# Eight of the feed-forward's column pairs by seven products instead of five, with the hidden pairs' low halves made by accumulating transfers

## The chip, the cores and the metric

The kernel runs on one core of a Trainium2 chip. The metric is device time in microseconds (us) of one execution; lower is better. The engines are named as in the profile: PE (TensorE, with PEld for its weight loads), DVE (VectorE), ACT (ScalarE), POOL (GpSimd) and SP (SyncE, which here only issues transfers).

## The reference, cut to what matters

One transformer-like layer on 512 tokens of 1024 features, in float32. Attention comes first; its code is the same in both kernels. The change lies in the convolutional gated feed-forward at the end:

```python
def conv_glu(x, w_up, conv_w, conv_b, w_down):      # x: (1, 512, 1024), w_up: (1024, 5632)
    hid = x @ w_up
    hid = lax.conv_general_dilated(hid, conv_w[:, None, :], ..., padding=((CONV_WIDTH - 1, 0),),
                                   feature_group_count=2 * D_FF) + conv_b
    gate, up = hid[..., :D_FF], hid[..., D_FF:]      # D_FF = 2816 columns each
    return (jax.nn.silu(gate) * up) @ w_down         # w_down: (2816, 1024)
```

## The kernel before

**Precision.** Every float32 operand is kept as two parts, `hi` (rounded to the matmul's format, cast by ACT) and `lo` (the rest, a subtraction on DVE). One product is three matmuls: hi by hi, hi by lo, lo by hi.

**Up-projection.** The 2816 gate columns and the 2816 up columns are cut into 22 column pairs of 128 + 128 (`up0` to `up21`). For each, SP loads 1 MB of weights into one of two slots (`raw`), ACT and DVE split them into `whi` and `wlo` (two buffers each), and PE multiplies them by the normalized tokens (`hth`, `htl`). While PE is at column pair j, the splits of j+1 are made and the load of j+3 is issued as soon as its slot is free (`run_chunk`, `split_gen`). An ordinary pair (`up_body`) is 48 matmuls of 512 columns (two outputs, eight slices of the features, three matmuls each). Five of the 22 pairs, those in `SEVEN`, are multiplied as 2x2 blocks by seven products instead of eight (`up_seven`): 84 matmuls of 256 columns. For this, four sums of the weight blocks are formed on DVE (`block_sums`, in `sx`) and split as well (`wxh`, `wxl`), and four sums of the token blocks are formed once and split (`token_sums`: the tiles `xT` and `ts`). The convolution, the gate and their product (`conv`, `gate`, `up_fin`) run on ACT and DVE while PE is at the next pair; the result of column pair j is one quarter of the tile `ub`.

**Hidden pairs.** Two column pairs make one hidden pair i (`pair_sums`). Its results are summed into blocks for a seven-product scheme of the down-projection, and split into `ax` (hi and lo, 1 MB) and `ay` (hi and lo, 768 KB): four sums on DVE, four casts on ACT, four subtractions on DVE. POOL then writes `ay` of the hidden pairs 0 to 6 out to DRAM (`ayd`) and reads them back after column pair 18 and in the down-projection (`fetch`).

**Down-projection.** `dn0_i` (24 matmuls with `ax` of hidden pair i) for all eleven hidden pairs, then `dn1_i` (18 matmuls with `ay`). 

**What sets the order.** The tile scheduler places the instructions of each engine in one fixed order; at run time an engine takes them in that order and waits on semaphores for the others. A transfer is queued by the engine that issues it, behind the waits in front of it there.

Of the kernel before, what the change touches and what calls it, by code (L numbers as in the profile page):

```python
# [8 lines left out]
F32 = mybir.dt.float32  # L9
# [53 lines left out]
SEVEN = (5, 8, 11, 14, 17)  # L63
# [3 lines left out]
def block_kernel(ctx: ExitStack, tc: tile.TileContext, x, xt, params, g2, rbx, wts, wd0, wd1, out):  # L67
# [45 lines left out]
    def load(i, parts=1):  # L113
# [6 lines left out]
        if i >= FIRST_DN:  # L120
            n = i - FIRST_DN
            if n < NP:
                SP.dma_start(raw, wd0[n])
            else:
                late["load"] = (SP.dma_start(raw[:, 0:1024], wd1[n - NP]),)
            yield
            return

        cuts = [0, *parts, 8] if isinstance(parts, tuple) else [8 * j // parts for j in range(parts + 1)]
        for a, b in zip(cuts, cuts[1:]):  # L130
            sl = slice(256 * a, 256 * b)
            SP.dma_start(raw[:, sl], wts[i, :, sl])
            yield
# [39 lines left out]
    def block_sums(i):  # L173

        b = raws[i].rearrange("p (b c) -> p b c", c=512)
        sx = late["pool"].tile([P, 1536], F32, tag="sx", name=f"sx_{order[i]}")
        late["sx"] = sx
        s1, s2, s4 = (sx[:, 512 * j:512 * (j + 1)] for j in range(3))
        V.tensor_tensor(s1, b[:, 1], b[:, 3], op=ALU.add)
        yield  # L180
        V.tensor_tensor(s2, s1, b[:, 0], op=ALU.subtract)
        yield
        V.tensor_tensor(s4, b[:, 2], s2, op=ALU.subtract)
# [4 lines left out]
    def split_seven(i, raw, hi, lo):  # L188

        key = order[i]  # L190
# [3 lines left out]
        sx = late["sx"]  # L194
        for j, (h, l, src) in enumerate(((hi[:, 0:1024], lo[:, 0:1024], raw[:, 0:1024]),
                                         (wh[:, 0:1024], wl[:, 0:1024], sx[:, 0:1024]),
                                         (hi[:, 1024:2048], lo[:, 1024:2048], raw[:, 1024:2048]),
                                         (wh[:, 1024:1536], wl[:, 1024:1536], sx[:, 1024:1536]))):
            A.copy(h, src)
            V.tensor_tensor(l, src, h.bitcast(F32), op=ALU.subtract)  # L200
            if j < 3:
                yield
# [39 lines left out]
    def run_chunk(key, body, pieces=4):  # L242

        sp = split_gen(pos[key] + 1, pieces)
        for _ in body(*splits.pop(key)):
            next(sp, None)
            yield
# [17 lines left out]
    ayd = dram.tile([7, P, 1536], F32, tag="ayd", name="ayd")  # L265

# [354 lines left out]

    def soft_b(h, t, ps):
# [247 lines left out]
    def pair_sums(i):  # L870
# [5 lines left out]
        if i < 8:  # L876
            ax = fp.tile([P, 2048], F32R, tag="ax", name=f"ax{i}", bufs=8)
            ay = fp.tile([P, 1536], F32R, tag="ay", name=f"ay{i}")
        elif i == 8:

            ax = fp.tile([P, 2048], F32R, tag="ts", name=f"ax{i}", bufs=4)
            ay = fp.tile([P, 1600], F32R, tag="wxh", name=f"ay{i}")[:, 0:1536]
            keep[0] = fp.tile([P, S], F32, tag="hg", name="t2_0")
# [367 lines left out]
```

## Time and profile before

| | |
|---|---|
| runs of the kernel | 725.96, 726.20, 726.39 us; median 726.2 us |
| the profiled execution | 726.66 us, of which the span from the first to the last instruction is 724.9 us |
| busy in the span | PE 718.6, PEld 627.5, DVE 565.4, ACT 401.5, POOL 53.6 us |
| granted PE clock | 1.00 of full speed |
| transfers | 100.91 MB, 139 GB/s over the span |

A busy time counts overlapping instructions once. PE's matmuls overlap each other, so their pace is read from the distance of their starts, not from the duration of one; the same holds, to a lesser degree, for DVE and ACT. In a row of the timeline stand the start, the duration, the engine, the line of the code, the operation with output and inputs, and how many instructions were merged. In a row of the stages stand the stage, its length, and for each engine the busy time and the number of instructions, then the granted clock, the transfer engines' share and GB/s.

### The profile page before, as it was taken

To read this page: it belongs to the slowest core of one execution; us is meant where nothing else is said; L and a number is where in the kernel's file an instruction comes from. 1 tells how busy PE (TensorE), PEld (TensorE's weight loads), DVE (VectorE), ACT (ScalarE), POOL (GpSimd) and SP (SyncE) were. 2 spreads that over 40 slices of the span, in tenths; PEclk is the share of its full clock that TensorE was granted. 3 is DMA by queue.
4 is the path that set the end of the run, shared out by engine and by line. 5 is a ranking of instruction groups with operands and counts; after the bars stand their busy time and mean duration, and the time that the engine had idled before them with its cause. 6 is when DMAs were issued, how large, how long until landed. Compare 5 with 4: busy or idle time off the path is not lost.

```text
span 724.9 us, 10589 instructions
## 1 busy us (share of the span) xinstructions
PE 718.6 (99%) x4019; PEld 627.5 (87%) x4019; DVE 565.4 (78%) x1030; ACT 401.5 (55%) x727; POOL 53.6 (7%) x95
## 2 busy tenths in 40 slices
PE   8999999999999999999999999999999999999997
PEld 8999998888988888888889889889898988888886
DVE  6678867775988888566275799998979985997686
ACT  6675656657767676442254556655545653543541
POOL 2701200000101011000012000000000100000000
PEclk9999999999999999999999999999999999999999
DMA  8632232211313111314536613544335553564563
GB/s 308 250 131 78 83 117 74 74 59 58 118 63 113 59 59 59 136 68 144 195 149 239 203 62 156 186 135 160 118 145 186 181 184 117 173 243 174 177 222 116
DMA packets 24786, 100.91 MB, mean 139 GB/s; under 512 B 2592, under 2 KB 7328, under 8 KB 17184
## 3 DMA queue, kind: packets, MB, share of 16 engines
q1 hardware_dynamic: 21792, 87.00, 33.8%
q0 software_dynamic: 2656, 13.11, 5.0%
q8 instruction: 31, 0.51, 0.3%
q14 instruction: 19, 0.16, 0.1%
q10 hardware_dynamic: 288, 0.14, 0.1%
HBM read 88.44 MB, written 11.80 MB: 138 GB/s over the span
## 4 chain that ended last, share of the span: by engine, by line
PE 98%; DMA 1%; SPq 0%; DVE 0%; ACT 0%; DVEq 0%; issue 0%
PE P L1087 14%; PE p L998 7%; PE pg L254 4%; PE pg L253 4%; PE pg L255 4%; PE pu L254 4%; PE pu L255 4%; PE pu L253 4%; PE qkB L255 2%; PE gB L255 2%; PE qkB L253 2%; PE gA L253 2%; PE gA L254 2%; PE gB L253 2%; PE gA L255 2%; PE qkB L254 2%
## 5 line engine op out<-in xcount | busy, mean ns | idle before, releaser
L253 PE MATMUL pg<-hth,whi_up 128*128 128x512 f32 (+1 forms) x152 | 55.7, 367 | 0.0
L255 PE MATMUL pg<-hth,wlo_up 128*128 128x512 f32 (+1 forms) x152 | 55.7, 366 | 0.0
L254 PE MATMUL pg<-htl,whi_up 128*128 128x512 f32 (+1 forms) x152 | 55.7, 366 | 0.0
L254 PE MATMUL pu<-htl,whi_up 128*128 128x512 f32 (+1 forms) x152 | 55.6, 366 | 0.0
L253 PE MATMUL pu<-hth,whi_up 128*128 128x512 f32 (+1 forms) x152 | 55.6, 366 | 0.0
L255 PE MATMUL pu<-hth,wlo_up 128*128 128x512 f32 (+1 forms) x152 | 55.6, 365 | 0.0
L1087 PE MATMUL P<-whi_dn,ax 128*128 128x512 f32 x176 | 54.4, 389 | 0.0
L149 ACT CAST whi_dn<-raw_dn 128x1024 fp32r<-128x1024 f32 x33 | 34.3, 1051 | 25.5 <-PE P L1087 15.2
L145 DVE TENSOR_TENSOR wlo_dn<-raw_dn,whi_dn 128x1024 fp32r<-128x1024 f32 x33 | 40.0, 1224 | 9.2 <-ACT whi_dn L149 9.1
L228 DVE TENSOR_TENSOR wlo_up<-raw_up,whi_up 128x1024 fp32r<-128x1024 f32 (+1 forms) x40 | 41.2, 1062 | 7.0 <-ACT whi_up L226 7.0
L226 ACT CAST whi_up<-raw_up 128x1024 fp32r<-128x1024 f32 (+1 forms) x40 | 34.5, 917 | 14.7 <-PE pu L254 7.9
L1087 PE MATMUL P<-whi_dn,ay 128*128 128x512 f32 x132 | 40.8, 389 | 0.0
L1087 PEld LDWEIGHTS P<-whi_dn,ax 128*128 128x128 f32 x176 | 33.0, 188 | 6.8
L1087 PE MATMUL P<-wlo_dn,ax 128*128 128x512 f32 x88 | 34.2, 389 | 0.0
L254 PEld LDWEIGHTS pu<-htl,whi_up 128*128 128x128 f32 x152 | 28.6, 188 | 4.7
L253 PEld LDWEIGHTS pu<-hth,whi_up 128*128 128x128 f32 x152 | 28.5, 188 | 4.7
L255 PEld LDWEIGHTS pg<-hth,wlo_up 128*128 128x128 f32 x152 | 28.6, 188 | 4.7
L255 PEld LDWEIGHTS pu<-hth,wlo_up 128*128 128x128 f32 x152 | 28.5, 188 | 4.6
L253 PEld LDWEIGHTS pg<-hth,whi_up 128*128 128x128 f32 x152 | 28.6, 188 | 4.6
L254 PEld LDWEIGHTS pg<-htl,whi_up 128*128 128x128 f32 x152 | 28.6, 188 | 4.5
L633 DVE TENSOR_TENSOR_SCAN aB<-aB,reset 128x127 f32<-128x127 f32 (+3 forms) x32 | 26.0, 817 | 6.7 <-ACT aB L628 6.7
L1087 PEld LDWEIGHTS P<-whi_dn,ay 128*128 128x128 f32 x132 | 24.8, 188 | 5.1
(303 smaller groups left out, 2240.3 us busy)
## 6 DMA issues: line engine op xcount, KB each, us to landing
raw_up<-in_wts SPq DMA_DIRECT2D x22, 1024.0 KB, 4.8
raw_dn<-in_wd SPq DMA_DIRECT2D x11, 1024.0 KB, 4.8
raw_dn<-in_wd SPq DMA_DIRECT2D x11, 512.0 KB, 3.4
ayd<-ay POOLq DMA_DIRECT2D x7, 768.0 KB, 5.2
ay<-ayd POOLq DMA_DIRECT2D x7, 768.0 KB, 6.5
raw_gA<-in_wts SPq DMA_DIRECT2D x4, 1024.0 KB, 4.7
raw_qkB<-in_wts SPq DMA_DIRECT2D x4, 1024.0 KB, 4.8
raw_gB<-in_wts SPq DMA_DIRECT2D x4, 1024.0 KB, 4.7
```

The lines of the kernel that those rows point to most:

```text
L145: chain("halves", V.tensor_tensor(o, x, y, op=op))
L149: chain("casts", A.copy(hi[:, sl], src))
L226: A.copy(hi[:, sl], raw[:, sl])
L228: E.tensor_tensor(lo[:, sl], raw[:, sl], hi[:, sl].bitcast(F32), op=ALU.subtract)
L253: PE.matmul(ps, sh, mh, start=first, stop=False)
L254: PE.matmul(ps, sh, ml, start=False, stop=False)
L255: PE.matmul(ps, sl, mh, start=False, stop=last)
L633: V.tensor_tensor_scan(ar, ar, reset[:, S - n:S - 1][:, ::-1], 1.0, op0=ALU.mult, op1=ALU.max)
L998: PE.matmul(ps, st, mv[:, k, :], start=first and k == 0 and n == 0, stop=last and k == 3 and n == 2, skip_group_check=True)
L1087: chain("products", PE.matmul(dst, st, mv, start=first and n == 0, stop=last and n == 2, skip_group_check=True))
```

## The change

Five things are changed together:

1. `SEVEN` is (6, 8, 10, 12, 14, 16, 18, 20) instead of (5, 8, 11, 14, 17): eight pairs, every second one from the seventh pair on. The splits of the token sums move from column pairs 2 and 3 to 3 and 4.
2. The sums of the weight blocks: only the first (`s1`) has a tile of its own; the other two are formed in place in `raw`, between the splits, so `raw` is read until the last of them.
3. For the hidden pairs 0 to 8 the low half is no longer a subtraction on DVE: ACT writes minus the rounded source into it, and POOL issues a transfer that adds the source onto it (`accum_op=ALU.add`): four such transfers for each hidden pair.
4. The steps of a hidden pair are taken one at a time (`late["todo"]`) along with the next column pair's products. `ay` has two buffers; it is written out by SP instead of POOL, ordered behind one more load of weights. `ax` of hidden pair 0 is written out too (`axd`), its buffer goes to hidden pair 8, and it is read back into another after column pair 20.
5. The reads of `ay` are spread over the down-projection: one after each of `dn0_0`, 2, 3, 5, 6, 8 and `dn1_0`, each waiting for the last load of weights to have landed.

```diff
-SEVEN = (5, 8, 11, 14, 17)
+SEVEN = (6, 8, 10, 12, 14, 16, 18, 20)
...
     def split_seven(i, raw, hi, lo):
...
-        for j, (h, l, src) in enumerate(((hi[:, 0:1024], lo[:, 0:1024], raw[:, 0:1024]),
-                                         (wh[:, 0:1024], wl[:, 0:1024], sx[:, 0:1024]),
-                                         (hi[:, 1024:2048], lo[:, 1024:2048], raw[:, 1024:2048]),
-                                         (wh[:, 1024:1536], wl[:, 1024:1536], sx[:, 1024:1536]))):
+        def part(h, l, c0, src):
+            sl = slice(c0, c0 + src.shape[-1])
+            A.copy(h[:, sl], src)
+            V.tensor_tensor(l[:, sl], src, h[:, sl].bitcast(F32), op=ALU.subtract)
+        part(hi, lo, 0, raw[:, 0:1024])
+        V.tensor_tensor(b[:, 0], s1, b[:, 0], op=ALU.subtract)
+        yield
+        part(wh, wl, 0, s1)
+        part(wh, wl, 512, b[:, 0])
+        yield
+        part(hi, lo, 1024, raw[:, 1024:2048])
+        V.tensor_tensor(b[:, 2], b[:, 2], b[:, 0], op=ALU.subtract)
+        yield
+        part(wh, wl, 1024, b[:, 2])
...
+    def after(ins, others):
+        for o in others:
+            tc.add_manual_dep(ins.ins, o.ins.name, mybir.DependencyInfo(
+                mybir.DependencyClass.Sync, mybir.DependencyReason.DATA), reason="paced")
+        return ins
...
                 A.copy(a[:, sl], src)
-                ins.append(V.tensor_tensor(a[:, n + o:n + sl.stop], src, a[:, sl].bitcast(F32), op=ALU.subtract))
+                if i < 9:
+                    A.activation(lo, src, AF.Copy, scale=-1.0)
+                    G.dma_start(lo, src, accum_op=ALU.add)
+                else:
+                    ins.append(V.tensor_tensor(lo, src, a[:, sl].bitcast(F32), op=ALU.subtract))
...
         if j % 2 == 1 and j // 2 < 9:
-            for step in pair_sums(j // 2):
-                step()
-            if j // 2 < 7:
-                G.dma_start(ayd[j // 2], pairs[j // 2][1].bitcast(F32))
+            i = j // 2
+            late["todo"] += [*pair_sums(i), *[lambda: None] * (6 if i else 0)]
+            if 0 < i < 8:
+                late["todo"].append(lambda: behind(SP.dma_start(ayd[i - 1], pairs[i - 1][1].bitcast(F32)), late["ld"]))
+            if i == 6:
+                late["todo"].append(lambda: behind(SP.dma_start(axd, pairs[0][0].bitcast(F32)), late["ld"]))
...
-            if j in (2, 3):
+            if j in (3, 4):
                 next(late["ts"])
...
-        if j == 18:
-            for i in range(5):
-                fetch(i)
+        if j == SEVEN[-1]:
+            keep[0] = fp.tile([P, S], F32, tag="hg", name="t2_0")
+            ax0 = fp.tile([P, 2048], F32R, tag="ts", name="ax0_", bufs=4)
+            G.dma_start(ax0, axd)
+            pairs[0] = (ax0, None)
...
+            n = ({0: 0, 2: 1, 3: 5, 5: 6, 6: 2, 8: 3}, {0: 4})[s].get(i)
+            if n is not None:
+                fetch(n)
```

How this moves the instructions is shown at three places. The line numbers of the changed kernel differ. In a name the digits next to the letters are the column pair or the hidden pair, those after the last underscore the buffer's.

DVE, at the end of a hidden pair, before (hidden pair 2, while PE is in column pair 7; `st` holds the sums, `L909` are the low halves):

```order
L898 TENSOR_TENSOR st2_4812<-ub_4184 128x256
L909 TENSOR_TENSOR ay2_4811<-ub_4184,ay2_4811 128x256
L899 TENSOR_TENSOR ub_4184<-ub_4184 128x256
L900 TENSOR_TENSOR st2_4812<-st2_4812,ub_4184 128x256
L853 SCALAR_TENSOR_TENSOR cg6_4860<-pg6_4826,par_88,cg6_4860 128x511
L909 TENSOR_TENSOR ax2_4810<-st2_4812,ax2_4810 128x256
L901 TENSOR_TENSOR st2_4812<-ub_4184,st2_4812 128x256
L909 TENSOR_TENSOR ax2_4810<-ub_4184,ax2_4810 128x768
L854 SCALAR_TENSOR_TENSOR cg6_4860<-pg6_4826,par_88,cg6_4860 128x510
L909 TENSOR_TENSOR ay2_4811<-st2_4812,ay2_4811 128x512
```

Sums and low halves alternate here. DVE, the same step now (hidden pair 3, while PE is in column pair 8, which is multiplied by seven products and gives `p6_8`, `p5_8`, `p7_8`):

```order
L1028 TENSOR_TENSOR hu8_4994<-p6_8_4991,hg8_4993 128x256
L939 TENSOR_TENSOR ub_4185<-cg7_4946,ub_4185 128x512
L903 TENSOR_TENSOR st3_5030<-ub_4185 128x256
L1034 TENSOR_TENSOR hg8_4993<-p5_8_4989,hu8_4994 128x256
L904 TENSOR_TENSOR ub_4185<-ub_4185 128x256
L905 TENSOR_TENSOR st3_5030<-st3_5030,ub_4185 128x256
L192 TENSOR_TENSOR wxl_up10_5143<-s1_up10_5049,wxh_up10_5142 128x512
L1038 TENSOR_TENSOR hu8_4994<-p7_8_4990,hu8_4994 128x256
L906 TENSOR_TENSOR st3_5030<-ub_4185,st3_5030 128x256
L1039 TENSOR_TENSOR hu8_4994<-hu8_4994,pc8_4992 128x256
```

The four subtractions into `ax` and `ay` are gone from DVE; the sums now stand between the additions that finish column pair 8.

ACT, at the same steps, before:

```order
L851 ACTIVATE ub_4184<-pu6_4827,par_88 128x512
L867 ACTIVATE cg5_4787<-cg5_4787 128x512
L908 CAST ay2_4811<-ub_4184 128x256
L851 ACTIVATE cg6_4860<-pg6_4826,par_88 128x512
L908 CAST ax2_4810<-st2_4812 128x256
L908 CAST ax2_4810<-ub_4184 128x768
L908 CAST ay2_4811<-st2_4812 128x512
L226 CAST whi_up9_5007<-raw_up9_4858 128x1024 x2
```

The four casts (`L908`) stand ahead of the casts of the next weights. ACT, now (`L914` is the cast to the high half, `L917` the negated write to the low half):

```order
L1031 COPY hg8_4993<-p1_8_4988 128x256
L191 CAST wxh_up10_5142<-s1_up10_5049 128x512
L914 CAST ay3_4987<-ub_4185 128x256
L917 ACTIVATE ay3_4987<-ub_4185 128x256
L914 CAST ax3_4986<-st3_5030 128x256
L917 ACTIVATE ax3_4986<-st3_5030 128x256
L861 ACTIVATE cg8_5103<-hg8_4993,par_88 128x512
L914 CAST ax3_4986<-ub_4185 128x768
L917 ACTIVATE ax3_4986<-ub_4185 128x768
L191 CAST whi_up10_5140<-raw_up10_4980 128x1024 x2
L914 CAST ay3_4987<-st3_5030 128x512
L917 ACTIVATE ay3_4987<-st3_5030 128x512
```

Each cast of a hidden pair has a second pass behind it, and the casts of column pair 10's weights (`whi_up10`) stand behind six of the eight.

SP, the loads of column pairs 8 to 14, before:

```order
L132 DMA raw_up8_4732<-in_wts 128x2048
L132 DMA raw_up9_4858<-in_wts 128x2048
L132 DMA raw_up10_4965<-in_wts 128x2048
L132 DMA raw_up11_5026<-in_wts 128x2048
L132 DMA raw_up12_5136<-in_wts 128x2048
L132 DMA raw_up13_5259<-in_wts 128x2048
L132 DMA raw_up14_5304<-in_wts 128x2048
```

Here SP issues nothing but loads. SP, the same loads now (`ayd` is the copy of `ay` in DRAM):

```order
L129 DMA raw_up8_4763<-in_wts 128x2048
L129 DMA raw_up9_4810<-in_wts 128x2048
L945 DMA ayd_108<-ay0_4439 128x1536
L129 DMA raw_up10_4980<-in_wts 128x2048
L945 DMA ayd_108<-ay1_4595 128x1536
L129 DMA raw_up11_5028<-in_wts 128x2048
L129 DMA raw_up12_5197<-in_wts 128x2048
L945 DMA ayd_108<-ay2_4770 128x1536
L129 DMA raw_up13_5250<-in_wts 128x2048
L945 DMA ayd_108<-ay3_4987 128x1536
L129 DMA raw_up14_5415<-in_wts 128x2048
```

The writes of `ay` stand between the loads, each behind the load that was issued last.

More of the change, by code (lines that the diff above doesn't have):

```diff
@@ L121, in load @@
             n = i - FIRST_DN
[L122 to L125, printed above, removed]
+            late["ld"] = (SP.dma_start(raw, wd0[n]) if n < NP else SP.dma_start(raw[:, 0:1024], wd1[n - NP]),)
             yield
@@ L175, in block_sums @@
         b = raws[i].rearrange("p (b c) -> p b c", c=512)
-        sx = late["pool"].tile([P, 1536], F32, tag="sx", name=f"sx_{order[i]}")
-        late["sx"] = sx
-        s1, s2, s4 = (sx[:, 512 * j:512 * (j + 1)] for j in range(3))
+        s1 = late["s1"] = late["pool"].tile([P, S], F32, tag="s1", name=f"s1_{order[i]}")
         V.tensor_tensor(s1, b[:, 1], b[:, 3], op=ALU.add)
[L180 to L183, printed above, removed]
         yield
@@ L1054, in block_kernel @@
             pass
-        if j == 18:
-            for i in range(5):
-                fetch(i)
+        if j == NF - 1:
+            for step in late["todo"]:
+                step()
+            late["todo"] = []
+        if j == SEVEN[-1]:
[3 more added lines that the diff above has]
+            pairs[0] = (ax0, None)
     BLK = {1: 0, 2: 1, 5: 2, 7: 3, 3: 0, 4: 1, 6: 2}
@@ L1179, in steps1 @@
         for t in range(NT):
-            behind(SP.dma_start(tmp["x"][t // 2][:, t % 2, :], x2d[t]), late["load"])
+            behind(SP.dma_start(tmp["x"][t // 2][:, t % 2, :], x2d[t]), late["ld"])
             if t in (1, 2):
```

45 lines of the change are left out of this document (21 added, 24 removed).

## The prediction, as it was put on record before the changed kernel was run

> **What bounds the kernel now.** I read the page first, then the chain of waits, then PE's starts in the feed-forward, then the busy times by stage, and last the starts on DVE and ACT, which tell what an instruction costs its engine.
>
> ```profile
> PE 718.6 (99%) x4019; PEld 627.5 (87%) x4019; DVE 565.4 (78%) x1030; ACT 401.5 (55%) x727; POOL 53.6 (7%) x95
> PE 98%; DMA 1%; SPq 0%; DVE 0%; ACT 0%; DVEq 0%; issue 0%
> ```
>
> PE is busy in 99% of the span and is 98% of the chain that ended last. Time goes only where PE's own work shrinks, and comes only where PE starts to wait. In the chain by time, a column pair with seven products is one piece:
>
> ```profile
> 435.60 9.89 PE p L998 x84
> 467.28 9.89 PE p L998 x84
> 498.96 9.89 PE p L998 x84
> 615.78 104.94 PE P L1087 x462
> ```
>
> It takes 9.89 us for 84 matmuls, 0.1177 each, three times alike. An ordinary pair follows from two starts, of column pairs 2 and 4:
>
> ```profile
> 402.77 0.40 PE L253 MATMUL pg<-hth,whi_up 128*128 128x512 f32 x1
> 424.56 0.39 PE L253 MATMUL pg<-hth,whi_up 128*128 128x512 f32 x1
> ```
>
> Two pairs take 21.79 us, one takes 10.895 (48 matmuls of 0.227). The chain's period agrees: 467.28 - 435.60 = 31.68 = 9.89 + 21.79, so PE waits nowhere between. By stage (one period, then its parts):
>
> ```profile
> 498.80:530.50 31.70, 31.70 (x182) 27.94 (x181) 28.65 (x45) 18.61 (x30) 1.07 (x2) 1.00 0.35 125
> 435.40:445.30 9.90, 9.90 (x85) 9.86 (x84) 9.90 (x16) 7.00 (x13) 0.54 (x1) 1.00 0.66 260
> 445.30:467.10 21.80, 21.80 (x98) 18.06 (x97) 21.80 (x37) 13.03 (x18) 0.53 (x1) 1.00 0.39 141
> ```
>
> The columns are PE, PEld, DVE, ACT, POOL. DVE is the next engine: full in the two stages around the first seven-product pair, 90% in a later period. The clock is 1.00.
>
> **The change part by part.** *Three more pairs by seven products* remove 3 x (10.895 - 9.89) = 3.02 us from PE. Where the pairs stand changes nothing in that. The Trainium skill, "TensorE: Matmul & The Clock Gate", section "Back-to-back issue gap", gives N/2.4 + 2.5 ns for a matmul of N columns in a stream; by it a pair would shrink from 48 x 215.8 to 84 x 109.2 ns, by 1.19 us, and the three by 3.56. The trace has 227 and 117.7 in their place, and the measured rows decide here.
>
> *DVE and ACT.* Costs are distances of starts in back-to-back rows:
>
> ```profile
> 445.46 0.43 DVE L899 TENSOR_TENSOR ub<-ub 128x256 f32<-128x256 f32 x1
> 445.79 0.43 DVE L900 TENSOR_TENSOR st<-st,ub 128x256 f32<-128x256 f32 x1
> 449.59 1.23 DVE L228 TENSOR_TENSOR wlo_up<-raw_up,whi_up 128x1024 fp32r<-128x1024 f32 x1
> 450.72 0.70 DVE L181 TENSOR_TENSOR sx_up<-sx_up,raw_up 128x512 f32<-128x512 f32 x1
> 451.33 0.70 DVE L185 TENSOR_TENSOR raw_up<-raw_up 128x512 f32<-128x512 f32 x1
> 457.00 0.76 DVE L853 SCALAR_TENSOR_TENSOR cg<-hg,par,cg 128x511 f32<-128x511 f32 x1
> 457.66 0.70 DVE L200 TENSOR_TENSOR wxl_up<-sx_up,wxh_up 128x512 fp32r<-128x512 f32 x1
> 460.72 1.24 DVE L200 TENSOR_TENSOR wlo_up<-raw_up,whi_up 128x1024 fp32r<-128x1024 f32 x1
> ```
>
> So 256 columns cost DVE 0.33, 512 cost 0.60, 1024 cost 1.13, and a convolution step 0.66. From column pair 6 on the pattern is one seven-product and one ordinary pair, 9.89 + 10.895 = 20.79 us of PE. In it DVE has, for the seven-product pair, four block sums (2.40), low halves of 2 x 1.13 + 3 x 0.60 (4.06), five small additions (1.65), four convolution steps (2.64) and one product (0.60): 11.35. The ordinary pair has 2.26 + 2.64 + 0.60 = 5.50, the hidden pair's four sums 1.32. Together 18.2 of 20.79, 87%. The hidden pair's low halves (0.33 + 0.33 + about 0.87 + 0.60 = 2.1, the 0.87 an estimate between the rows of 512 and 1024) are off DVE; with them it would have been 20.3, no room. ACT:
>
> ```profile
> 442.93 0.41 ACT L908 CAST ay<-ub 128x256 fp32r<-128x256 f32 x1 [1.43 <-DVE ub L928]
> 443.25 0.78 ACT L851 ACTIVATE cg<-pg,par 128x512 f32<-128x512 f32 x1
> 445.92 0.84 ACT L908 CAST ax<-ub 128x768 fp32r<-128x768 f32 x1 [0.92 <-DVE ub L899]
> 446.66 1.99 ACT L226 CAST whi_up<-raw_up 128x1024 fp32r<-128x1024 f32 x2
> 448.56 0.62 ACT L867 ACTIVATE cg<-cg 128x512 f32<-128x512 f32 x1
> 449.09 0.60 ACT L908 CAST ay<-st 128x512 fp32r<-128x512 f32 x1
> ```
>
> These cost it 0.32, about 0.68, 0.74, 0.95 each of two, and 0.53. The four negated writes are taken as the casts: 2 x 0.32 + 0.74 + 0.53 = 1.91 for each hidden pair, 17 us in nine. The seven-product pair costs ACT 2 x 0.95 + 3 x 0.53 for casts, 4 x 0.32 for copies out of PE's banks (an estimate by the cast of 256 columns), 2 x 0.68 and 0.53 for convolution and gate, 6.7; the ordinary pair 1.90 + 1.36 + 0.53 = 3.8; the hidden pair's casts 1.9. That is 14.3 of 20.79. Neither engine bounds, so both edits cost nothing, as long as the splits come in time. Laying the new order's rows one behind another with these costs, DVE ends the last low half of column pair 10's weights 1.6 us before PE starts that pair, that of the second block sum (needed 36 matmuls into the pair, 4.2 us) 2.8 before: PE is about 7 us from waiting. Before the change the low half of column pair 8 ended at 460.72 + 1.24 = 461.96, 5.3 us ahead of 467.28.
>
> *Token sums one pair later.* Their use is one pair later too: 0.
>
> *Block sums in place.* A weight slot is now read until the last of them. First sum to last low half is 13.9 us of DVE's rows in the new order, then the load:
>
> ```profile
> raw_up<-in_wts SPq DMA_DIRECT2D x22, 1024.0 KB, 4.8
> DMA to landing us min/median/max: 4.6/4.8/8.8
> ayd<-ay POOLq DMA_DIRECT2D x7, 768.0 KB, 5.2
> DMA to landing us min/median/max: 3.5/5.3/9.0
> htd<-xf_n POOLq DMA_DIRECT2D x5, 256.0 KB, 2.5
> L933 POOL DMA_DIRECT2D ayd<-ay x7: 533/533/542, 438.8 to 553.9; - x7
> ```
>
> (The first landing line is that of the weight loads, the second that of `ay` in both directions.) 13.9 + 4.8 = 18.7 us in a period of 20.79: it holds up to a load of 6.8. I take the median, 4.8, since in the new order nothing large runs beside these loads. Ends: 4.6 costs 0, 8.8 is the first rival.
>
> *Writes of `ay` by SP.* Eight transfers enter SP's queue, each issued after a load and ahead of the next. They wait for sums that are a column pair or more old, so SP does not stand, and the next load waits for its slot, not for them. ACT's `ay` of hidden pairs 3 and 4 waits for the write of 1 and 2: load and write, 4.8 + 5.2 = 10.0 us behind the slot's release at -1.6, so 8.4 us into the column pair, where ACT is at about 8.2. A delay under 2 us twice, inside the 7: 0. POOL loses the seven old writes.
>
> *Accumulating transfers.* No row shows one. POOL issues 36, at 0.53 us 19 us, with nothing else queued behind them until column pair 20. They land before anyone needs them if they take up to 13.7 us: the next hidden pair's sums rewrite `st` 20.79 later, and about 7.1 of that are DVE's and ACT's rows up to the write that the transfer follows. Bounds are 2.5 (the 256 KB row, the size of the largest one from `st`) and 9.0 (the worst of 768 KB): 0 at both ends.
>
> *`ax` of hidden pair 0* is read back over a column pair before `dn0_0`, 17 us or more ahead of its use: 0 at 9.0. *Reads of `ay`.* The last, of hidden pair 4, is issued when the load in this row has landed:
>
> ```profile
> 679.00 0.33 SPq L125 DMA_DIRECT2D raw_dn<-in_wd  x1
> raw_dn<-in_wd SPq DMA_DIRECT2D x11, 512.0 KB, 3.4
> 684.00:688.00 4.00, 4.00 (x20) 3.30 (x19) 3.38 (x6) 1.49 (x3) 0.00 (x0) 1.00 0.67 251
> 688.00:692.00 4.00, 4.00 (x19) 3.31 (x18) 2.83 (x4) 1.53 (x2) 0.00 (x0) 1.00 0.75 269
> ```
>
> That is at 682.4; it lands 5.3 to 9.0 later, at 687.7 to 691.4. PE needs it at 615.78 + 336 x 0.2271 = 692.1. Both move by -3. It is hidden, narrowly, beside transfers that keep the engines 67 to 75% busy. 0, with the upper end in the third rival.
>
> Sum: 726.66 (the profiled execution's own time) - 3.02 = 723.6; that execution lies 0.46 above the median of the runs, 726.2, so the runs should have 723.2.
>
> **The rivals.** *(1) The weight slot's loop is too long.* For: loads beside other transfers took up to 8.8; the accumulations add traffic. Against: the median is 4.8, and in the new order they are issued 5 us and more ahead of these loads. Each us over 6.8 costs DVE 1 us in each of seven periods, and PE pays what goes beyond 7. At 8.0 that is 8.4 - 7 = 1.4, so 724.6; at 8.8 it is 7.0, so 730.2. It turns the sign at 8.2.
>
> *(2) Slower: the accumulations land late.* One mechanism: DVE stands at the first sum of the next hidden pair until the last transfer out of `st` has landed, and everything behind it with it. Each us over 13.7 costs six periods 1 us. For: an accumulation also reads what it writes to, and no row prices that. Against: the worst row is 9.0 for three times the bytes. At twice that, 18.0, it is 26 - 7 = 19, so 742. It turns the sign at 15.4.
>
> *(3) The last `ay` comes late* for `dn1_4`. At 10.5 us it is 0.8 late, so 724.0; the whole gain is gone only at 12.7.
>
> *(4) The new pairs run faster than the old.* Matmuls of 256 columns also stand in column pairs 0 and 1, whose last 46 are 45 distances of 0.1133:
>
> ```profile
> 397.56 0.28 PE L254 MATMUL pg<-htl,whi_up 128*128 128x256 f32 x1
> 402.66 0.28 PE L255 MATMUL pu<-hth,wlo_up 128*128 128x256 f32 x1
> ```
>
> At that pace a pair takes 9.52, the three save 4.1, and the time is 722.1. Against it stand the 9.89 of each old seven-product pair, whose code for PE is the same.
>
> *(5) Nothing gained:* three new pairs that PE spends waiting as long as it saves, 726.2. DVE full in the stage of the first such pair speaks for it, the load of 87% after the edit against.
>
> **How the numbers follow.** About 0.2% (1.5 us) is what a measurement of this kernel can tell from no change. My forecast has 0.70. Rival 1 has 0.10 (0.03 still faster, 0.03 the same, 0.04 slower), rival 2 0.08 (0.01 the same, 0.07 slower), rival 3 0.07 (0.05 faster, 0.02 the same), rival 4 0.02, rival 5 0.03. That makes faster 0.80, same 0.09, slower 0.11. The range is 722.1 (rival 4) to 725.5 (the lower part of rivals 1 and 3); it leaves out rival 2, rival 5 and the upper part of 1.
>
> **What would show it.** Right: eight pieces of 84 matmuls and 9.89 us in the chain of waits, 20.79 apart, no release of PE by DVE, ACT or a transfer in the up-projection, and the down-projection's 104.9 us unchanged. Wrong: a start-to-start distance over 20.79 with DVE low halves as what PE waits for (rivals 1 and 2; a wait of DVE for a weight load or for a transfer out of `st` tells which), or a gap in front of `dn1_4` (rival 3).

## Result, and the profile after

The changed kernel takes 735.1 us (median of 5 executions, 731.5 to 735.6) against 726.4 us before (725.96 to 726.94): ratio 1.0104, 95% interval 1.0077 to 1.0132. It is slower by 1%; 723.2 was forecast. (The ratio compares all executions with those of the kernel before that ran beside them, so it is not the quotient of the two medians.) The profiled execution took 735.61 us, its span is 733.6.

On the page of the kernel after, first the busy times, then the chain that ended last by engine:

```profile
PE 718.4 (98%) x4127; PEld 630.4 (86%) x4127; DVE 565.9 (77%) x1035; ACT 426.4 (58%) x789; POOL 81.7 (11%) x125
PE 73%; DMA 9%; DVE 8%; issue 7%; ACT 1%; POOL 1%; SPq 0%; DVEq 0%; POOLq 0%; ACTq 0%
```

PE's share of the chain fell from 98 to 73%, although it is busy in 98% of the span. A quarter of the chain is now transfers, DVE and "issue" (time in which the profile shows no reason for a wait). The transfers are of two kinds, by line `ay<-st` (4% of the span) and the loads of weights, `raw_up<-in_wts` (4%). Pieces of that chain in order of time:

```profile
478.49 9.80 DMA ay<-st
488.42 0.44 DVE st L903
...
500.00 9.92 DMA ay<-st
510.04 0.42 DVE st L903
...
563.82 9.89 DMA ay<-st
573.83 0.43 DVE st L903
...
603.36 5.66 PE p L1013 x48
609.48 4.09 PE p L1013 x36
624.02 105.33 PE P L1109 x462
```

Instead of pieces of 84 matmuls there are three accumulating transfers of nearly 10 us, each followed by the first sum of the next hidden pair. The down-projection takes 105.33 us (104.94 before): it is not there that time went. The start of the up-projection and of the down-projection, before and then after, bound the stage (columns: start, duration, instruction):

```profile
378.93 0.28 PE L253 MATMUL pg<-hth,whi_up 128*128 128x256 f32 x1
615.62 0.39 PE L1087 MATMUL P<-whi_dn,ax 128*128 128x512 f32 x1
```
```profile
381.07 0.28 PE L255 MATMUL pg<-hth,whi_up 128*128 128x256 f32 x1
623.86 0.39 PE L1109 MATMUL P<-whi_dn,ax__6407 128*128 128x512 f32 x1
```

The up-projection has 242.79 us now and had 236.69: 6.10 more, where 3.02 less was forecast, so 9.12 us are to be explained there. Another 2.14 us were lost ahead of it, in code that the change doesn't touch. What PE waited for in the up-projection (total, times, longest), and what DVE waited for:

```profile
PE p L1013 <- ACT hg L1018: 5.5, 5, 2.5
PE p L1013 <- DVE wlo_up L192: 1.1, 1, 1.1
PE pg L255 <- ACT whi_up L226: 0.7, 1, 0.7
PE p L1013 <- DVE wxl_up L192: 0.5, 1, 0.5
```
```profile
DVE st L903 <- DMA ay<-st: 12.7, 5, 6.4
DVE s_up L174 <- DMA raw_up<-in_wts: 7.8, 7, 1.8
```

PE's 7.8 us are most of the 9.12, and the rest is in the counting: a wait is taken from the modelled end of the matmul ahead, 0.28 us or more after its start, where the pace is 0.12 or 0.23. By distances of starts, less that pace, the same eight waits take 9.1 us. Five of the eight waits are for one instruction that the prediction never placed: ACT's copy `hg<-p` (L1018), which takes the first result out of bank b1 before PE may add its fifth product there. DVE's largest wait is the one of rival 2, behind the last transfer out of `st`. How the two hang together shows in POOL's rows, then in ACT's and PE's:

```profile
427.79 0.91 POOL L918 DMA_DIRECT2D ay<-ub  x1 [32.73 <-DVE ub L864]
430.80 0.87 POOL L918 DMA_DIRECT2D ax<-st  x1 [2.09 <-DVE cg L864]
433.84 0.85 POOL L918 DMA_DIRECT2D ax<-ub  x1 [2.17 <-DVE wlo_up L228]
...
470.67 0.84 POOL L918 DMA_DIRECT2D ax<-ub  x1 [4.47 <-ACT ay L917]
475.20 0.88 POOL L918 DMA_DIRECT2D ay<-ub  x1 [3.69 <-DVE wxl_up L192]
478.49 0.85 POOL L918 DMA_DIRECT2D ay<-st  x1 [2.41 <-ACT whi_up L226]
```
```profile
470.90 0.63 ACT L917 ACTIVATE ay<-st 128x512 fp32r<-128x512 f32 x1
...
499.01 0.78 ACT L861 ACTIVATE cg<-pg,par 128x512 f32<-128x512 f32 x1 [1.33 <-DVE ub L939]
499.69 1.98 ACT L226 CAST whi_up<-raw_up 128x1024 fp32r<-128x1024 f32 x2
501.57 0.78 ACT L861 ACTIVATE ub<-pu,par 128x512 f32<-128x512 f32 x1
502.25 0.36 ACT L1018 COPY hg<-p 128x256 f32<-128x256 f32 x1
```
```profile
502.67 0.39 PE L1013 MATMUL p<-hth,whi_up 128*128 128x256 f32 x1 [2.48 <-ACT hg L1018]
```

An accumulating transfer keeps POOL busy 0.86 us, and the next one starts 3.0 us after it at the earliest. The releasers in brackets don't explain that: the negated write behind the second row was done at 428.57, behind the third at 430.42. The time from issue to landing does (the trace gives it to a tenth of a us). Six of the transfers, one after another:

| transfer | issued | lands after | landed | next one issued |
|---|---|---|---|---|
| `ay<-ub` | 427.79 | 2.7 | 430.5 | 430.80 |
| `ax<-st` | 430.80 | 2.7 | 433.5 | 433.84 |
| `ax<-ub` | 433.84 | 8.4 | 442.2 | 442.51 |
| `ax<-ub` | 470.67 | 4.2 | 474.9 | 475.20 |
| `ay<-ub` | 475.20 | 3.0 | 478.2 | 478.49 |
| `ay<-st` | 478.49 | 9.8 | 488.3 | 488.60 |

Of 35 successors 31 go out 0.3 us after the transfer ahead of them has landed, and none sooner. None of them waits for the semaphore of the one ahead; what they wait for is, but for a few waits on DVE, the same as for the plain copies of e2_plain below. So the 36 transfers run one at a time: their landings sum to 162 us, with 35 x 0.3 to 173 of the 182 us between the first issue and the last landing. That is 19.2 us for each of nine hidden pairs, which follow one another every 20.79, and leaves almost no room. The negated write of `ay<-st` was done at 471.5; its transfer is fourth in the queue, goes out at 478.5 and lands at 488.3. DVE stands 2.59 us, until 488.42, at the sums of the next hidden pair; a stand of 1.72 us for a load of weights, until 482.60, lies shortly ahead of it. From there to 499.5 its rows follow one another without a gap. Its lateness reaches ACT at 499.01 (1.33 us for the product `ub`), the copy stands behind 3.2 us of ACT's other rows, and PE waits 2.48 us for it.

### The profile page after: what moved, and what is told of

The parts are those of the page before. It is cut to its first block, busy times and chain, and to the rows that moved or that the text cites. A ratio compares the mean times of both kernels' runs of the same rounds, so it can differ in the third digit from the quotient of the medians.

```text
span 733.6 us, 11019 instructions
## 1 busy us (share of the span) xinstructions
PE 718.4 (98%) x4127; PEld 630.4 (86%) x4127; DVE 565.9 (77%) x1035; ACT 426.4 (58%) x789; POOL 81.7 (11%) x125
## 4 chain that ended last, share of the span: by engine, by line
PE 73%; DMA 9%; DVE 8%; issue 7%; ACT 1%; POOL 1%; SPq 0%; DVEq 0%; POOLq 0%; ACTq 0%
PE P L1109 14%; DMA ay<-st 4%; DMA raw_up<-in_wts 4%; PE qkB L257 2%; PE gB L257 2%; PE qkB L255 2%; PE gA L255 2%; PE gA L256 2%; PE gB L255 2%; PE gA L257 2%; PE qkB L256 2%; PE gB L256 2%; PE wo L257 2%; PE wo L255 2%; PE wo L256 2%
## 5 line engine op out<-in xcount | busy, mean ns | idle before, releaser
L146 ACT CAST whi_dn<-raw_dn 128x1024 fp32r<-128x1024 f32 x33 | 34.5, 1052 | 27.3 <-DMA raw_dn<-in_wd 13.7
L255 PE MATMUL pg<-hth,whi_up 128*128 128x512 f32 (+1 forms) x128 | 46.5, 364 | 0.7 <-ACT whi_up L226 0.7
L257 PE MATMUL pg<-hth,wlo_up 128*128 128x512 f32 (+1 forms) x128 | 46.4, 362 | 0.0
L256 PE MATMUL pg<-htl,whi_up 128*128 128x512 f32 (+1 forms) x128 | 46.3, 362 | 0.0
L256 PE MATMUL pu<-htl,whi_up 128*128 128x512 f32 (+1 forms) x128 | 46.3, 362 | 0.0
L255 PE MATMUL pu<-hth,whi_up 128*128 128x512 f32 (+1 forms) x128 | 46.3, 362 | 0.0
L257 PE MATMUL pu<-hth,wlo_up 128*128 128x512 f32 (+1 forms) x128 | 46.2, 361 | 0.0
L228 DVE TENSOR_TENSOR wlo_up<-raw_up,whi_up 128x1024 fp32r<-128x1024 f32 (+1 forms) x34 | 33.6, 1030 | 3.0 <-ACT whi_up L226 3.0
L226 ACT CAST whi_up<-raw_up 128x1024 fp32r<-128x1024 f32 (+1 forms) x34 | 28.5, 892 | 7.0 <-issue 3.6
L645 POOL TENSOR_SCALAR_AFFINE_SELECT bB<-bB 128x128 f32<-128x128 f32 x32 | 13.6, 428 | 149.2 <-DVE bB L644 134.5
L674 ACT CAST pth_A<-pT_A 128x128 fp32r<-128x128 f32 (+2 forms) x40 | 14.7, 372 | 22.4 <-PE pT_A L661 14.7
```

Source lines behind the costliest of these rows:

```text
L146: chain("casts", A.copy(hi[:, sl], src))
L226: A.copy(hi[:, sl], raw[:, sl])
L228: E.tensor_tensor(lo[:, sl], raw[:, sl], hi[:, sl].bitcast(F32), op=ALU.subtract)
L255: PE.matmul(ps, sh, mh, start=first, stop=False)
L256: PE.matmul(ps, sh, ml, start=False, stop=False)
L257: PE.matmul(ps, sl, mh, start=False, stop=last)
```

## The experiments

The theories: **A**, the accumulating transfers (A1 the adding itself, A2 any four more transfers on that queue, A3 a type conversion in them); **B**, eight seven-product pairs are too dense for DVE and ACT; **C**, the spills (SP's writes of `ay` to DRAM) behind the loads slow the weights' loads; **D** and **E**, what makes the start-up 2 us longer; **F**, the spills lengthen the landings of the accumulating transfers. The expectations still price a transfer at 3.0 us, the shortest distance; that it is the landing which sets it is read from the table above. All results in one table; "up-projection" is between the two rows shown above, "starts" is the first of them. These two and the waits come from one profiled execution of each kernel, the medians from 4 to 12. The kernel before ran beside each of the others; its row is that of the first comparison. e2_plain and e11_small compute something else, as said below; of e11_small only the up-projection counts.

| kernel | median us | ratio to before, interval | up-projection us | starts at us | PE waits in it us |
|---|---|---|---|---|---|
| before | 726.4 | | 236.69 | 378.93 | 0 |
| after | 735.1 | 1.0104 (1.0077 to 1.0132) | 242.79 | 381.07 | 7.8 |
| e1_dve | 728.49 | 1.0024 (1.0014 to 1.0034) | 234.47 | 379.69 | 0.3 |
| e2_plain | 725.87 | 0.9995 (0.9985 to 1.0006) | 233.55 | 379.93 | 0 |
| e3_ub | 727.06 | 1.0006 (0.9997 to 1.0014) | 235.11 | 381.46 | 1.0 |
| e4_five | 738.66 | 1.0152 (1.0126 to 1.0177) | 249.21 | 378.49 | 8.4 |
| e5_f32 | 732.83 | 1.0103 (1.0082 to 1.0123) | 241.03 | 379.56 | 6.1 |
| e6_st | 726.52 | 1.0005 (0.9997 to 1.0014) | 234.12 | 379.83 | 0 |
| e7_pool | 746.48 | 1.0282 (1.0265 to 1.0300) | 251.29 | 381.24 | 14.0 |
| e8_order | 728.90 | 1.0042 (1.0030 to 1.0055) | 238.95 | 379.39 | 4.4 |
| e9_large | 725.87 | 0.9997 (0.9987 to 1.0008) | 234.45 | 379.18 | 0.4 |
| e10_seven | 727.71 | 1.0015 (1.0005 to 1.0025) | 234.80 | 379.16 | 0 |
| e11_small | 749.77 | 1.0314 (1.0296 to 1.0333) | 239.20 | 379.61 | 4.4 |
| b1_axd | 726.27 | 1.0002 (0.9994 to 1.0011) | 236.69 | 378.98 | 0 |
| b2_pad | 727.00 | 1.0011 (1.0002 to 1.0020) | 237.47 | 378.22 | 0.7 |

**e1_dve: the low halves back on DVE.**

```
-                if i < 9:
+                if False:
```

> The changed kernel with the low halves of all hidden pairs subtracted on DVE again, so no negated write on ACT and no accumulating transfer on POOL; all else of the change stays. If the accumulating transfers cost the time (theory A), PE's waits in the up-projection fall from 7.8 us to under 2 and the time is 723 to 726 us, although DVE is then asked for 20.3 of 20.79 us. If eight seven-product pairs are simply too dense for DVE and ACT (theory B), it gets worse than the changed kernel: 735 to 740 us, with DVE low halves as what PE waits for. If the spills behind the weight loads slow the loads (theory C), DVE still waits for weight loads and the time stays at 731 to 735 us.

728.5 us, between A's and B's numbers. In the up-projection A holds: 234.47 us, 2.22 less than before. The loss is behind it: DVE, asked for 20.3 of 20.79 us, ends the last product of the up-projection 6.3 us after the first matmul of the down-projection (4.3 in e2_plain), and PE waits twice there for a low half of its weights:

```profile
PE P L1109 <- DVE wlo_dn L142: 2.2, 2, 1.3
```

From the start of the down-projection to the end of the span it takes 112.5 us where the kernel before takes 109.3: 3.3 us lost. So eight pairs fit in the up-projection even so; B holds only past its end.

**e2_plain: the same transfers without the adding.**

```
-                    G.dma_start(lo, src, accum_op=ALU.add)
+                    G.dma_start(lo.bitcast(F32), src)
```

> The changed kernel with each accumulating transfer turned into a plain copy of the same source to the same place by the same queue; the low halves then hold the copied sums and not the rest, so that part of the computation is changed. If it is the adding that is dear (theory A1), POOL issues these at 0.53 us each, close together, the copies land in 2 to 4 us, DVE does not stand at the first sum of a hidden pair, and the time is 723 to 726 us. If it is four more transfers per hidden pair on that queue beside the loads, adding or not (theory A2), or the density (B) or the spills (C), it stays at 731 to 735 us.

POOL's rows and the chain of this kernel, and the landings of one group:

```profile
442.92 0.54 POOL L918 DMA_DIRECT2D ax<-st  x1 [2.64 <-DVE ub L863]
444.39 0.55 POOL L918 DMA_DIRECT2D ax<-ub  x1 [0.94 <-ACT ax L917]
445.43 0.54 POOL L918 DMA_DIRECT2D ay<-st  x1 [0.50 <-DVE ub L864]
```
```profile
468.14 9.89 PE p L1013 x84
488.94 9.91 PE p L1013 x84
...
613.64 105.04 PE P L1109 x462
```
```profile
ay<-st POOLq DMA_DIRECT2D x9, 256.0 KB, 3.2
```

Plain copies go out as little as 0.64 us apart (1.04 in the last two of these rows), 17 of 35 before the one ahead has landed, and those out of `st` land in 3.2 (median); DVE stands once behind one, for 0.2 us, and PE nowhere. The up-projection is 3.14 us shorter than before, as the sum in the prediction said (3.02), and 9.24 shorter than in the changed kernel: A1, the adding, is the whole loss there. A2, B and C fall for the up-projection, since all that they blame is still in this kernel. (That the destination is given as fp32 here changes nothing, see e5_f32.) Its time is only 725.87, 2.7 over the forecast 723.2: it starts 1.0 us later, and its executions spread from 723.7 to 728.4.

**e3_ub: only the pieces out of the products by transfer.**

```
-                if i < 9:
+                if i < 9 and o == 0:
```

> The changed kernel with only the pieces out of the products (two per hidden pair) by accumulating transfer; the two pieces out of the single-buffered sums are subtracted on DVE, so no transfer reads that tile. If DVE's stand behind the last transfer out of the sums is what makes PE wait (theory A), DVE waits for no transfer there and the time is 724 to 727 us, with DVE asked for 19.1 of 20.79 us. If POOL's pace alone or the density (B) matters, or the spills (C), it is 730 us or more.

727.06 us, just past the upper end of A. DVE waits for no transfer at L903, and PE has a single wait:

```profile
PE pg L255 <- DVE cg L864: 1.0, 1, 1.0
```

**e6_st: only the two pieces out of the sums by transfer** (`o > 0`).

> The mirror of the run with the pieces out of the products: here only the two pieces out of the single-buffered sums go by accumulating transfer, the two out of the products are subtracted on DVE. If what delays the release of the sums is that four transfers stand one behind another on POOL at 3.0 us each, two take 6 us, DVE's stands behind them go down to under 3 us in all and the time is 725 to 728 us. If it is the landing of the transfer itself (up to 9.9 us beside the other traffic), DVE stands as in the changed kernel (about 12 us in all) and the time is 730 to 735 us.

As the first branch has it: the transfer that stalled DVE in the changed kernel is still there, but second in a row and not fourth, and DVE's stands are one of 1.4 us:

```profile
DVE st L903 <- DMA ay<-st: 1.4, 1, 1.4
```
```profile
ay<-st POOLq DMA_DIRECT2D x9, 256.0 KB, 3.3
```

It lands in 3.3 us (median) where the changed kernel has 5.5. All landings of this kernel sum to 64 us of 166: the chain of transfers has room, and neither this transfer nor its size is dear by itself.

**e8_order: all four by transfer, those out of the sums first.**

```
-                    G.dma_start(lo, src, accum_op=ALU.add)
+                    d = G.dma_start(lo, src, accum_op=ALU.add)
+                    t["acc"] = (behind(d, t.get("acc", ())),)
...
+        return (sums, lambda: halves(ax, ((768, t["st"][:, 0:256]),)) + halves(ay, ((256, t["s42"]),)),
+                lambda: halves(ax, ((0, u[:, 0:768]),)) + halves(ay, ((0, u[:, 768:1024]),)))
```

> The changed kernel with all 36 accumulating transfers kept, but the two out of the single-buffered sums issued first on POOL and the two out of the products behind them. If DVE stands because the last transfer out of the sums is fourth in a row of transfers that POOL issues 3.0 us apart, it is now second, DVE's stands behind it go down from 12.7 us to under 4 us and the time is 726 to 729 us. If the sum of the transfers' work is at fault, wherever each stands, it stays at 731 to 736 us.

728.9 us. With the same 36 transfers, their order, and with it that of the casts and negated writes on ACT, brings back 3.84 of the 9.24 us:

```profile
DVE st L903 <- DMA ay<-st: 4.0, 3, 1.6
```
```profile
PE p L1017 <- ACT hg L1022: 4.4, 3, 2.1
```

PE still waits for ACT's copy. The place in POOL's queue is part of the cause. The chain of transfers itself is as full as before (landings of 173 us in 187), so the sums are freed earlier but not early enough.

**e5_f32: the destination given as plain fp32.** `G.dma_start(lo.bitcast(F32), src, accum_op=ALU.add)`

> The changed kernel with the destination of each accumulating transfer given as plain fp32, like its source, so that the transfer adds and converts nothing. If the dear part is the conversion between source and destination types (theory A3), POOL's issue falls to about 0.53 us, the landings to 2 to 4 us, and the time to 724 to 728 us, as with the plain copies. If it is the adding (theory A1), POOL still spends 0.86 us on each and stands about 2 us behind it, and the time stays at 731 to 736 us.

A3 falls: POOL's busy time is the same (858 ns for this group here and in the changed kernel), the ratio is 1.0103 against 1.0104, and DVE stands 10.7 us behind these transfers against 12.7.

```profile
L918 POOL DMA_DIRECT2D ay<-st x9 | 7.7, 858 | 34.5 <-ACT whi_up L226 12.6 <-ACT whi_up L191 7.6 <-ACT cg L861 6.9
```

**e4_five: five seven-product pairs, all else of the change.** `SEVEN = (6, 9, 12, 15, 18)`

> The changed kernel with five seven-product pairs (6, 9, 12, 15, 18) and all else of the change: accumulating transfers, spills by SP, sums in place. PE's work is then that of the kernel before. If accumulations cost by landing late (theory A), a hidden pair has 21.8 or 31.7 us for about 12 us of POOL, half of its stands go, and the time is 727 to 730 us. If the density of eight pairs is at fault (B), PE waits nowhere and it is 726 us. If the spills are (C), DVE waits for loads as before and it is 728 us or more.

B falls outright: with PE's work of before it is the slower kernel, 738.7 us, and its up-projection is 12.5 us longer than before. It is also 9 us over what I expected of A, and that expectation was wrong about the room: a hidden pair comes with every two column pairs, 20.8 or 21.8 us in either kernel, never 31.7.

```profile
DVE st L903 <- DMA ay<-st: 16.6, 5, 6.2
DVE s_up L174 <- DMA raw_up<-in_wts: 16.1, 4, 5.6
```

The landings sum to 177 us of 195, with 8 of them over 7 us (5 in the changed kernel). Why more of them are long here isn't settled. PE's waits, 8.4 us, take 9.9 by distances of starts; after the one of 2.05 us that ends at 523.68 its granted clock is down to 0.50 from 526 to 528 us (1.00 in the changed kernel throughout the up-projection), and the matmuls from 523 to 531 us lose another 1.7.

**e7_pool: POOL subtracts the low halves.** `ins.append(G.tensor_tensor(lo, src, a[:, sl].bitcast(F32), op=ALU.subtract))`

> The changed kernel with the low halves of the hidden pairs subtracted by POOL instead of negated by ACT and accumulated by a transfer. From the 1.30 us that a 512-column subtraction took on POOL, four pieces take about 4.6 us of a period of 20.79, so by theory A (the accumulating transfers alone are at fault) PE waits under 2 us in the up-projection and the time is 723 to 726 us, and DVE is asked for 18.2 of 20.79. If the density of eight pairs is at fault (B), 730 us or more.

A miss: 746.5 us. POOL's subtractions slow DVE's. In the up-projection of this kernel, one group of DVE and one of POOL (columns: count | busy us, mean ns of one):

```profile
L192 DVE TENSOR_TENSOR wxl_up<-s_up,wxh_up 128x512 fp32r<-128x512 f32 x7 | 16.1, 2301 | 0.2 <-ACT wxh_up L191 0.2
```
```profile
L917 POOL TENSOR_TENSOR ax<-ub,ax 128x768 fp32r<-128x768 f32 x9 | 18.4, 2050 | 1.2 <-ACT ax L914 1.2
```

A 512-column subtraction of two operands takes DVE 0.68 us elsewhere in the same stage and 2.30 here, where each of the seven ran beside POOL's subtraction of 768 columns. The Trainium skill, "GPSIMD Engine Reference", section "1. Specifications", says that POOL shares its SBUF interfaces with DVE and that they contend when a DVE instruction has two inputs in SBUF; the trace agrees. The expectation left that out.

**e11_small: spills of an eighth of the bytes.** The long landings have traffic beside them. SP's issues around the transfer of 478.49:

```profile
476.12 0.33 SPq L129 DMA_DIRECT2D raw_up<-in_wts  x1
476.54 0.41 SPq L945 DMA_DIRECT2D ayd<-ay  x1
480.25 19.61 SPq L129 DMA_DIRECT2D raw_up<-in_wts  x2
```

A load of 1 MB, a spill of 768 KB and another load are issued within 4.1 us. The edit leaves SP's order alone:

```
-behind(SP.dma_start(ayd[i - 1], pairs[i - 1][1].bitcast(F32)), late["ld"])
+behind(SP.dma_start(ayd[i - 1][:, 0:192], pairs[i - 1][1][:, 0:192].bitcast(F32)), late["ld"])
```

> The changed kernel with each spill of ay cut to its first 192 of 1536 columns, at the same place of SP's queue; the down-projection reads these columns back eight times over, so that part of the computation is changed, and its time says nothing here. All 36 accumulating transfers stay. If the long landings come from the spill that runs beside a weight load (theory F), none is over 7 us but the one beside the write of axd, DVE's stands at the first sums go from 12.7 us to under 5, PE's waits from 7.8 to under 4, and the up-projection from 242.8 to 235 to 239 us. If the weight loads alone lengthen them, or only the transfers' number counts, landings of 9 us and more remain and the up-projection stays at 241 to 244 us.

The up-projection takes 239.20 us, just above F's range and below the other branch's: 3.6 of the 9.1 us to explain come from the spills' bytes. F as written misses its other marks too: five of the 36 landings are over 7 us (five in the changed kernel), PE waits 4.4 us, DVE's stands are 7.2:

```profile
DVE st L903 <- DMA ay<-st: 7.2, 2, 6.5
```

6.5 of these are one stand, behind a transfer that stood behind a landing of 8.5 us, beside weight loads alone (the first spill is issued 17 us after that landing). The same stand is the longest in the changed kernel, 6.4 us, again ahead of any spill. So spills and loads both lengthen the landings, and theory C was right in this roundabout way: the spills cost nothing with plain copies, and a good third of the loss with accumulating ones.

**b1_axd and b2_pad: the start-up.** b1 is the kernel before with the scratch tensor `axd` and its write, b2 the kernel before with 62 `G.memset` in each of seven column pairs.

> The kernel before with the change's scratch tensor for hidden pair 0 added in device memory and written once by SP behind the work of column pair 13; nothing reads it. The profiled execution of the changed kernel started 2 us later into its second stage, with a granted clock of 0.68 to 0.90 between 8 and 16 us, and most executions of the variants so far show a mean clock of 0.995 to 0.998, those of the kernel before 0.999 or more. If the new tensor's place in memory causes that (theory D), some of these executions show it too and are 1.5 to 2 us longer, median 726.5 to 728. If not, they are as before: 726.2 us, all at 0.999 or more.

> The kernel before with 434 small fills on POOL added in the feed-forward, where POOL is idle, so that the program has as many instructions as the changed kernel; they write a tile that nobody reads. The variants with eight seven-product pairs moved 197 to 225 GB/s from 4 to 8 us of the span, those with five 269 to 283, and start 1 to 2 us later into the up-projection. If the length of the program causes that (theory E), this kernel shows it: under 230 GB/s there and a median of 727 to 728.5 us. If not, it is 726.2 us, with 270 to 285 GB/s.

The first loads and PE's granted clock (the column ahead of the DMA share), in the kernel before, after, and in b2:

```profile
4.00:8.00 4.00, 3.04 (x19) 2.27 (x18) 2.31 (x5) 2.03 (x5) 0.67 (x2) 1.00 0.89 283
8.00:12.00 4.00, 4.00 (x35) 3.93 (x35) 3.89 (x8) 3.98 (x9) 0.00 (x0) 1.00 1.05 392
```
```profile
4.00:8.00 4.00, 3.07 (x16) 2.45 (x14) 2.65 (x4) 1.18 (x2) 0.66 (x2) 1.00 0.95 220
8.00:12.00 4.00, 2.93 (x15) 2.93 (x16) 2.75 (x6) 3.38 (x8) 0.00 (x0) 0.68 1.05 394
```
```profile
4.00:8.00 4.00, 3.54 (x17) 2.91 (x16) 2.80 (x5) 1.91 (x4) 0.67 (x2) 1.00 0.80 265
```

After, the loads from 4 to 8 us move 220 GB/s and not 283, PE stands, and its clock goes down to 0.68. The order of the instructions on every engine is the same there in all these kernels. Neither the scratch tensor (281 GB/s, 726.27 us) nor the length of the program (265 GB/s, start at 378.22) does that: D and E fall. b2 is slower for another reason, a wait of PE of 0.7 us in the up-projection and a down-projection 0.9 us longer. D and E rest on one profiled execution each, and on medians that stay within 0.11% of before.

**e9_large and e10_seven: the two larger pieces by transfer** (`src.shape[-1] > 256`), with eight and with seven seven-product pairs.

> The changed kernel with only the two larger pieces of a hidden pair (768 columns out of the products, 512 out of the sums) by accumulating transfer and the two of 256 columns subtracted on DVE, which is then asked for 18.9 of 20.79 us. By the pace of 3.0 us a transfer, two of them leave no stand: no wait of PE, an up-projection as short as with the plain copies (233.6 us from its first product to the first one of the down-projection), and 725 to 727 us; what the slower start-up of the variants with eight seven-product pairs takes is in that. If the larger pieces are dear by their bytes, DVE stands again behind the one out of the sums and it is 729 us or more.

> The run with the two larger pieces by accumulating transfer, with seven seven-product pairs instead of eight (column pair 20 is ordinary again). PE has 1.0 us more to do than with eight, so its up-projection should take 235.5 us. What is open is the slower start-up of the variants with eight (197 to 225 GB/s from 4 to 8 us): if it comes with every longer program of PE, it stays here (under 230 GB/s) and the time is 726 to 727 us; if it comes only with eight, these executions start as the kernel before (270 GB/s and more) and the time is 725 us or less.

e9's time is as expected, 725.87 us; its up-projection of 234.45 is 0.85 longer than expected, with one wait of PE of 0.4 us. Within its interval it is no different from before. e10 misses: 241 GB/s from 4 to 8 us, between the two branches, and 727.7 us, slower than before by 0.15% although no wait of PE shows in its up-projection. Its executions spread from 725.8 to 729.6, the profiled one took 725.86.

## Why the prediction was wrong

**The step that failed: "*Accumulating transfers.* ... POOL issues 36, at 0.53 us 19 us, with nothing else queued behind them until column pair 20", put at "0 at both ends".** It took the issue of a plain write for that of an accumulating one and asked only how long one takes to land, with the landings of plain transfers. Measured: 0.86 us on POOL each, and the next one only when it has landed. Four of a hidden pair take 2.7 + 2.7 + 3.9 + 3.3 and four times 0.3, 13.8 us, by the shortest landings of each size, and 19.2 on average beside loads and spills. "Nothing else queued behind them" overlooked that they queue behind one another: the one that frees `st` was last. A single landing stayed near the bound I had (9.9 at worst against 9.0); the bound of 13.7 counted from ACT's write, and there 7 us of the queue (471.5 to 478.5) came on top.

**"PE is about 7 us from waiting" was mis-sized.** The slack was that of the low halves. In a seven-product pair PE needs ACT's copy out of b1 by its fifth product, 48 matmuls or 5.65 us into the pair, and on ACT it stands behind casts and convolutions that wait for DVE. The first stand, 6.4 us at 445.90, already cost PE 3.1 us of waits between 449.96 and 458.44, the one of 2.6 at 488.42, with 1.7 for a load ahead of it, 2.5. By these rows the slack is, as an estimate, 3 us at the one place and 2 at the other, not 7.

**Rival 2 had the place and not the mechanism.** DVE stood at the first sum of the next hidden pair, as it said; but the transfer was late mainly because up to three others had to land ahead of it. It took one landing of 15.4 us for the turn of the sign; none was over 9.9. At 8% it was far too unlikely: "no row prices that" was a reason for a wide range, and bounds out of rows of plain transfers are not bounds of an operation that does something else.

**What held.** The 3.02 us on PE (3.14 with plain copies). Casts and negated writes on ACT, sums in place, token sums a pair later, SP's writes: all are in e2_plain, where PE waits nowhere. DVE was asked for 18.2 of 20.79 us; in two periods of e2_plain (from 488.94 and from 530.52) it is busy for 18.7 and 20.1, and still holds nothing up. Rival 1: loads rose from 4.8 to 6.4 us (medians), DVE waited 7.8 us for them after and 8.9 in e2_plain, and there it cost PE nothing; in the changed kernel these waits add to the stands behind the transfers, and what part of the 9.1 us they carry is not separated. SP's writes took 7.8 us, not 5.2; by themselves they hid. The last `ay` hid: the down-projection's piece is 105.3 us after and 105.0 in e2_plain, 104.94 before. One citation was inexact: the Trainium skill, "TensorE: Matmul & The Clock Gate", section "Back-to-back issue gap", gives N/2.4 + 2.5 ns for an isolated matmul, not for one in a stream; the sum went by the measured 0.227 and 0.1177 us, so nothing hung on it.

**What the sum did not contain.** The kernels with seven or eight seven-product pairs start the up-projection at 379.2 to 381.5 us, those before and b1 and b2 at 378.2 to 379.0, and the instructions ahead of it are the same in all. Three of those executions (after, e3_ub, e7_pool) start past 381, and they are the three whose granted clock is down, to 0.68 to 0.73, from 8 to 12 us; in the others it is 1.00. For the changed kernel that is 2.1 of its 8.7 us of span. It is not shown what causes it; the scratch tensor and the length of the program did not bring it about, and e4_five, with five such pairs, started at 378.49.

## What to carry to other kernels

A transfer that adds is another operation than a copy: where the trace has no row of it, ask whether the next one may start before it has landed, and if that is not known, put the landings of all that share the queue one behind another before asking when the last of them frees its source. Slack is to be taken at every instruction that PE waits for, copies out of its banks included, and not at the weights alone. Here two of the four pieces by transfer, in each of the three choices tried (e3_ub, e6_st, e9_large), gave the time of before back; the gain on PE was real, but no version gave it to the whole time.

## What the runs showed of the hardware

Accumulating transfers on POOL's queue ran one at a time: in five kernels with all four pieces by such transfers, each went out 0.3 us or more after the one ahead had landed, mostly just 0.3, whether its destination was fp32 or fp32r. Plain copies in their place overlapped (0.54 us of POOL each, down to 0.64 us apart), and a plain read of 1 MB went out 1.27 us after an accumulating transfer that landed 4.9 us after its issue. At the shortest they landed in 2.6 us for 128 KB, 3.3 for 256 and 3.9 for 384, where plain copies took 1.9, 2.2 and 2.5; at the longest in 11.9, a piece of 384 KB in e4_five beside a spill, the write of `axd` and loads. The Trainium skill, "DMA: Bandwidth & Descriptors", section "SWDGE vs HWDGE vs iDMA", has accumulation as a feature of POOL's queue alone, where software writes the descriptors; no run here tried another queue. POOL's subtractions of 256, 512 and 768 columns took 0.97, 1.84 and 2.05 us and a DVE subtraction of 512 columns beside the largest took 3.4 times as long (2.30 us for 0.68, mean of seven).
